# HGRN and retention on one Trainium2 core: k scaled on GpSimd, level 32 copied by ScalarE, the retention gate on GpSimd, head outputs transposed later

## The chip, the core and the metric

The kernel runs on one core of a Trainium2 chip. The core has TensorE (PE, with its weight loads PEld), VectorE (DVE), ScalarE (ACT), GpSimd (POOL) and SyncE (SP, which issues most DMAs). Each engine works through its own list of instructions in order and waits on semaphores for the others. The metric is the device time of one execution in microseconds, the median of several runs.

## What is computed

One layer of a decoder trunk over 1024 positions of width 1024, all in float32: a token-mixing sub-layer (an HGRN2 gated linear recurrence with 8 heads and a retention branch with 4 heads, merged by gates) and a squared-ReLU MLP, each with a residual and a layer norm. The change touches the two recurrent branches:

```python
def _hgrn2(q, zf, v, g, lb):
    q = jax.nn.silu(q)
    log_f = jnp.logaddexp(jnp.log(lb), jnp.log1p(-lb) + jax.nn.log_sigmoid(zf))
    k = (1.0 - lb) * jax.nn.sigmoid(-zf)
    ...
        b = jnp.cumsum(lfc, axis=2)
        rel = jnp.where(causal, b[:, :, :, None, :] - b[:, :, None, :, :], -jnp.inf)
        scores = jnp.einsum('bhid,bhijd,bhjd->bhij', qc, jnp.exp(rel), kc)
        o = scores @ v + (qc * jnp.exp(b)) @ state
        state = exp(b_last) * state + (kc * jnp.exp(b_last - b))^T @ vc
    o = _head_norm(o, centered=False)
    return o * jax.nn.silu(g)

def _retention(q, k, v, g, positions):
    ...
    o = _head_norm(o, centered=True)
    return o * jax.nn.silu(g)

def _head_norm(o, centered):
    if centered:
        o = o - jnp.mean(o, axis=-1, keepdims=True)
    return o * lax.rsqrt(jnp.mean(jnp.square(o), axis=-1, keepdims=True) + HEAD_NORM_EPS)
```

## The kernel before

**Order of the work.** The kernel is one Python trace over tiles. Projections (`dense_T`, helpers `split` and `mm3` at L181 to L188) split each float32 operand into a high and a low part (ACT makes the high, DVE the low part) and multiply three times on PE. The order in which each engine executes its list is settled at compile time by a planner that starts an instruction when, by its own prices for operations, the inputs are ready; it can therefore put a few projection products between two steps of a recurrence. On the chip each list is then in order. In the program's text, generators give the coarse order: `weave` and `mix` alternate the steps of the recurrence (`h_rec`, one `yield` a step) with steps of projections (`h_fill`, later `r_first`). `later(n, fn)` puts a piece of work off by n steps, and `tick`, once a step, runs what is due.

**HGRN.** There are four pairs of heads (p = 0 to 3). For each head `h_rec` keeps k, transposed, as a tile of 128 channels x 1024 positions (named `fk`), q in three versions (`hq`), and builds the 128 x 128 score blocks of eight chunks in S without a cumulative sum: first the pairs of neighbours (L815 to L819), then three levels of sizes 2, 8 and 32 (`H_SIZES`), each of which scores the quarters of a block of 4 x size against each other. One level is:

- L840 and L841 make the moving operand X (tile `U`) from the query product of the level before; L843 and L844 make the products of the decays (tiles `D`);
- four banks of matmuls (L851, two chunks each; the weights are k, the moving operand is X) into PSUM tiles `psa`, of which there are two;
- for each bank three masked copies from PSUM into S (L858, `copy_predicated`, on DVE);
- L861 and L862 scale parts of k by decays for the next level, L863 and L864 do so for X.

Before the levels L824 makes X's query part and L827 scales the even positions of k. After the last level the head goes through its two halves of four chunks: k is transposed (L874) and copied by ACT (L876), the outputs are formed from S and the state (L885, L886), copied by ACT (L887) and squared (L888), and the state is updated (L891, DVE at L896). At the end of a half POOL raises the mean square to the power -1/2 (L901, with `rs` as output), ACT scales the four output blocks (L903), and `h_out` is put off by `H_DEFER[p // 3]` steps: it transposes the half (L911, bank `psb`), multiplies by the gate on DVE (L913) and stores it by a DMA that POOL issues (L914, `oh_d`). `h_merge` reads `oh_d` after the last pair.

**Retention.** `r_head` runs over eight blocks of 128 positions for each of four heads: the state's matmuls (L1105), its high and low parts (ACT and DVE, tiles `fk`), the output's matmuls (L1119), a copy with a scale (L1121), and `r_norm`: statistics on DVE (L1142 to L1144), the power on POOL (L1145), (output - mean) x gate in one DVE instruction (L1146), the scale by the power on ACT (L1147). Three steps later `r_out` transposes the block (L1154), copies it (L1156) and POOL issues its store (L1157). Head 0 runs beside the gate projections, head 1 starts during the last HGRN pair, heads 1 to 3 run beside the merge of the HGRN output (`r_fill`).

Two rows of other places are used for prices: L1221, a product of two SBUF tiles on POOL in the last merge, and L1302, a 128x1 operation on DVE in the norm of the output projection, behind a power on POOL at L1240.

Of the kernel before, what the change touches and what calls it, by code (L numbers as in the profile page):

```python
# [14 lines left out]
AF = mybir.ActivationFunctionType  # L15
ALU = mybir.AluOpType
# [3 lines left out]
P = 128  # L20
# [35 lines left out]

ADA_ORDER = [(s, g) for s in (S_GATE2, S_GATE1, S_SCALE2, S_SHIFT2) for g in range(4)]

H_DEFER = (3, 8)


def constants():
# [70 lines left out]
class Trunk:  # L133
# [666 lines left out]
    def h_rec(self, p, hd):  # L800
        nc = self.nc
        h = 2 * p + hd
        s = self.hst[p][hd]
        q, f, k, v = s["q"], s["f"], s["k"], s["v"]
        S = [self.hS[(2 * h + hf) % len(self.hS)] for hf in (0, 1)]
        V = nc.vector
        fv = f.rearrange("p (b two) -> p two b", two=2)
        V.tensor_tensor(q[:, 2], q[:, 1], fv[:, 1], op=ALU.mult)
        yield

        for bk in range(4):
            pa = self.ps("a", (P, 384)).rearrange("p (c w b) -> p c w b", c=2, w=3)
            for c in (0, 1):
                n = 2 * bk + c
                nc.tensor.matmul(pa[:, c], k[:, n * P:(n + 1) * P], q[:, :, n * 64:(n + 1) * 64], start=True, stop=True)  # L815
            Sv = S[bk // 2][:, bk % 2 * 2:bk % 2 * 2 + 2, :].rearrange("p c (b two) -> p c two b", two=2)
            mk = self.mask8[:, :P].rearrange("p (b two) -> p two b", two=2).unsqueeze(1).to_broadcast([P, 2, 2, 64])
            V.copy_predicated(Sv, mk, pa[:, :, 0:2])
            V.copy_predicated(Sv[:, :, 1], self.mask8[:, P:P + 64].unsqueeze(1).to_broadcast([P, 2, 64]), pa[:, :, 2])  # L819
            if bk == 1:  # L820
                yield
        X = self.hX
        qp = X[:, 0]
        V.tensor_tensor(qp.rearrange("p (b two) -> p two b", two=2), q[:, 0::2],  # L824
                        fv[:, 0].unsqueeze(1).to_broadcast([P, 2, T // 2]), op=ALU.mult)
        ke = k.rearrange("p (b two) -> p two b", two=2)[:, 0]
        V.tensor_tensor(ke, ke, fv[:, 1], op=ALU.mult)  # L827
        Dt = self.hD[hd]
        V.tensor_tensor(Dt, fv[:, 0], fv[:, 1], op=ALU.mult)


        for ln, sz in enumerate(H_SIZES):
            B = T // (4 * sz)
            Xv = X.rearrange("p w (b f s) -> p w f b s", f=4, s=sz)
            kv = k.rearrange("p (b f s) -> p f b s", f=4, s=sz)
            Dv = Dt.rearrange("p (b f) -> p f b", f=4)
            D2 = self.xp.tile([P, 2 * B], F32, tag=f"D{2 * ln + 1}", bufs=1, name=self.uid("D"))
            D4 = self.xp.tile([P, B], F32, tag=f"D{2 * ln + 2}", bufs=1, name=self.uid("D"))
            by = lambda d, *sh: (d if len(sh) == 2 else d.unsqueeze(1).to_broadcast([P, 2, B])).unsqueeze(len(sh)).to_broadcast([P, *sh])
            V.tensor_tensor(Xv[:, 1, 2], Xv[:, 0, 3], by(Dv[:, 2], B, sz), op=ALU.mult)  # L840
            V.tensor_tensor(Xv[:, 1, 1::2], Xv[:, :, 2], by(Dv[:, 1], 2, B, sz), op=ALU.mult)  # L841
            D2v = D2.rearrange("p (b two) -> p two b", two=2)
            V.tensor_tensor(D2v, Dv[:, 0::2], Dv[:, 1::2], op=ALU.mult)  # L843
            V.tensor_tensor(D4, D2v[:, 0], D2v[:, 1], op=ALU.mult)  # L844
            yield
            for bk in range(4):
                pa = self.ps("a", (P, 384))
                for c in (0, 1):
                    n = 2 * bk + c
                    mv = X[:, :, n * P:(n + 1) * P].rearrange("p w (b r) -> p b w r", r=4 * sz)[:, :, :, sz:]  # L850
                    nc.tensor.matmul(pa[:, c * 192:(c + 1) * 192].rearrange("p (b w r) -> p b w r", w=2, r=3 * sz),  # L851
                                     k[:, n * P:(n + 1) * P], mv, start=True, stop=True)
                pv = pa.rearrange("p (b w r s) -> p b w r s", w=2, r=3, s=sz)
                Sv = S[bk // 2][:, bk % 2 * 2:bk % 2 * 2 + 2, :].rearrange("p c (b f s) -> p (c b) f s", f=4, s=sz)
                for j, (dst, src) in enumerate(((Sv[:, :, 1::2], pv[:, :, 0, 0::2]), (Sv[:, :, 2:4], pv[:, :, :, 1]),
                                                (Sv[:, :, 2:4], pv[:, :, 1, 0::2]))):
                    o = P + 64 + 384 * ln + 128 * j
                    V.copy_predicated(dst, self.mask8[:, o:o + 128].rearrange("p (b two s) -> p b two s", two=2, s=sz), src)  # L858
                if bk == 1:
                    yield  # L860
            V.tensor_tensor(kv[:, 0::2], kv[:, 0::2], Dv[:, 1::2].unsqueeze(3).to_broadcast([P, 2, B, sz]), op=ALU.mult)  # L861
            V.tensor_tensor(kv[:, 0:2], kv[:, 0:2], by(D2v[:, 1], 2, B, sz), op=ALU.mult)  # L862
            V.tensor_tensor(Xv[:, 0, 1], Xv[:, 0, 1], by(Dv[:, 0], B, sz), op=ALU.mult)  # L863
            V.tensor_tensor(Xv[:, 0, 2:4], Xv[:, :, 2], by(D2v[:, 0], 2, B, sz), op=ALU.mult)  # L864
            Dt = D4
        yield
        state = None
        for hf in (0, 1):
            g = self.e2()
            nc.sync.dma_start(g, self.hg_d[h][:, hf * 512:hf * 512 + 512])  # L870
            pb = self.ps("b")
            for c in range(4):
                cs = slice(hf * 512 + c * P, hf * 512 + c * P + P)
                nc.tensor.transpose(pb[:, c * P:(c + 1) * P], k[:, cs], self.ident)  # L874
            kt = self.e2()
            nc.scalar.activation(kt, pb, AF.Copy)  # L876
            ob, sq = (self.e2().rearrange("p (c e) -> p c e", c=4) for _ in (0, 1))
            ms = self.xp.tile([P, 4], F32, tag="ms", bufs=2, name=self.uid("ms"))
            for c in range(4):
                n = 4 * hf + c  # L880
                cs = slice(n * P, n * P + P)
                vn = v[:, n, hd * P:(hd + 1) * P]
                po = self.ps("c", (P, P))
                if n > 0:
                    nc.tensor.matmul(po, qp[:, cs], state, start=True, stop=False)  # L885
                nc.tensor.matmul(po, S[hf][:, c, :], vn, start=n == 0, stop=True)  # L886
                nc.scalar.activation(ob[:, c, :], po, AF.Copy)  # L887
                nc.scalar.activation(sq[:, c, :], ob[:, c, :], AF.Square, accum_out=ms[:, c:c + 1])  # L888
                if n < 7:
                    pu = self.ps("c", (P, P))  # L890
                    nc.tensor.matmul(pu, kt[:, c * P:(c + 1) * P], vn, start=True, stop=True)  # L891
                    ns = self.xp.tile([P, P], F32, tag="st", bufs=2, name=self.uid("st"))
                    if n == 0:
                        nc.vector.tensor_copy(ns, pu)
                    else:
                        nc.vector.scalar_tensor_tensor(ns, state, Dt[:, n:n + 1], pu, op0=ALU.mult, op1=ALU.add)  # L896
                    state = ns
                yield
            nc.vector.tensor_scalar(ms, ms, 1.0 / P, HEAD_EPS, op0=ALU.mult, op1=ALU.add)
            rs = self.xp.tile([P, 4], F32, tag="rs", bufs=2, name=self.uid("rs"))  # L900
            nc.gpsimd.tensor_tensor(rs, ms, self.mhalf[:, :4], op=ALU.pow)  # L901
            for c in range(4):
                nc.scalar.activation(ob[:, c, :], ob[:, c, :], AF.Copy, scale=rs[:, c:c + 1])  # L903
            self.later(H_DEFER[p // 3], lambda ob=ob, hf=hf, g=g: self.h_out(h, hf, ob, g))
            yield
# [232 lines left out]
    def r_norm(self, h, n, of, g):  # L1138
        nc, V = self.nc, self.nc.vector
        stat = self.xp.tile([P, 16], F32, tag="stat", bufs=2, name=self.uid("stat"))  # L1140
        b6, mv, rs = stat[:, 0:6], stat[:, 8:10], stat[:, 12:13]
        V.bn_stats(b6, of)  # L1142
        V.bn_aggr(mv, b6)
        V.tensor_scalar(rs, mv[:, 1:2], HEAD_EPS, None, op0=ALU.add)  # L1144
        nc.gpsimd.tensor_tensor(rs, rs, self.mhalf[:, :1], op=ALU.pow)  # L1145
        V.scalar_tensor_tensor(of, of, mv[:, 0:1], g, op0=ALU.subtract, op1=ALU.mult)  # L1146
        nc.scalar.activation(of, of, AF.Copy, scale=rs)  # L1147
        self.later(3, lambda: self.r_out(h, n, of))

    def r_out(self, h, n, of):  # L1150
# [574 lines left out]
```

## Time and profile before

| what | us |
|---|---|
| time, median of 3 runs | 2324.97 |
| lowest and highest | 2318.06, 2326.09 |
| the profiled execution | 2319.84 |
| its span, first to last instruction | 2318.1 |

| engine | busy in the span | share |
|---|---|---|
| PE matmul | 2250.6 | 97% |
| PE weight loads | 1851.3 | 80% |
| DVE | 1652.0 | 71% |
| ACT | 1008.7 | 44% |
| POOL | 294.6 | 13% |

The profile is of one execution. A row of a group of instructions names the line of the kernel, the engine, the operation, the output and input tiles, the shape and the count; behind the bar stand the busy time, the mean length of one in ns, and how long the engine stood idle just before them, with what ended that. A row of a timeline has the start, the length, the engine and line, and in brackets the idle time before it. Matmuls overlap in the pipeline, so the lengths of single ones add up to more than the time that they take, and a busy PE isn't PE at its peak. The HGRN recurrence occupies about 884 to 1240 us of the span, retention heads 1 to 3 about 1240 to 1460 us.

### The profile page before, as it was taken

The page shows a single profiled execution, that of the slowest core. Times are in us where ns is not written, and L with a number is a line of the kernel's source. Part 1 is how long each engine was busy: PE and PEld are TensorE (multiplying, and loading weights), DVE is VectorE, ACT ScalarE, POOL GpSimd, SP SyncE. Part 2 cuts the span into 40 slices and gives each one's busy share as a digit, 9 for nine tenths or more (in the row PEclk, how much of TensorE's full clock was granted, in tenths as well). Part 3 has the DMA queues.
Part 4 walks back from the last instruction along what each step waited for, and adds up shares of the span by engine and source line. Part 5 has one row for each costly group of instructions (what it writes and reads, how often), then busy time and mean ns, then how long its engine had stood idle before and what let it go on. Part 6 is the DMA issues. An engine that isn't in the chain of part 4 may idle for free.

```text
span 2318.1 us, 29884 instructions
## 1 busy us (share of the span) xinstructions
PE 2250.6 (97%) x10366; PEld 1851.3 (80%) x10366; DVE 1652.0 (71%) x3078; ACT 1008.7 (44%) x1829; POOL 294.6 (13%) x460
## 2 busy tenths in 40 slices
PE   6999999999999999999989999999989999999997
PEld 5888888888888788778877788888878888788886
DVE  7866768676777556778876667667886666668669
ACT  4433435443333352432435556222465555643441
POOL 0111010111111120010011222013012111100001
PEclk9999999999999999999999999999999999999999
DMA  9676655433333441122234666864244444777653
GB/s 287 220 229 219 224 195 200 159 129 108 116 109 112 164 150 60 42 91 63 75 104 156 236 193 211 297 212 154 95 145 164 154 152 152 283 254 241 211 168 127
DMA packets 227415, 385.86 MB, mean 166 GB/s; under 512 B 17480, under 2 KB 122688, under 8 KB 226496
## 3 DMA queue, kind: packets, MB, share of 16 engines
q1 hardware_dynamic: 197232, 285.95, 38.7%
q0 software_dynamic: 29712, 97.55, 11.3%
q8 instruction: 82, 1.34, 0.2%
q14 instruction: 69, 0.57, 0.1%
q10 hardware_dynamic: 320, 0.45, 0.1%
HBM read 282.17 MB, written 101.72 MB: 166 GB/s over the span
## 4 chain that ended last, share of the span: by engine, by line
PE 62%; issue 23%; DVE 6%; DMA 3%; POOL 3%; ACT 2%; SPq 0%; ACTq 0%; POOLq 0%; DVEq 0%
PE psd L187 11%; PE psd L186 11%; PE psd L188 11%; PE psa L188 3%; PE psa L187 3%; PE psa L186 3%; PE psc L187 3%; PE psc L186 3%; PE psc L188 3%; PE psb L1119 2%; PE psc L1105 1%; PE psb L186 1%; PE psb L187 1%; PE psb L188 1%; DVE U L182 1%
## 5 line engine op out<-in xcount | busy, mean ns | idle before, releaser
L186 PE MATMUL psd<-U,wh 128*128 128x512 f32 x760 | 305.1, 403 | 2.1 <-ACT wh L181 1.5
L187 PE MATMUL psd<-U,wh 128*128 128x512 f32 x760 | 303.8, 400 | 1.4 <-DVE U L182 1.4
L188 PE MATMUL psd<-U,wl 128*128 128x512 f32 x760 | 303.4, 399 | 0.0
L181 ACT ACTIVATE bh<-s 128x512 fp32r<-128x512 f32 x204 | 128.3, 633 | 248.3 <-PE psd L187 61.1
L186 PE MATMUL psd<-U,bh 128*128 128x512 f32 x496 | 193.8, 391 | 2.1 <-DVE e L449 2.1
L188 PE MATMUL psd<-U,bl 128*128 128x512 f32 x496 | 193.7, 390 | 0.0
L187 PE MATMUL psd<-U,bh 128*128 128x512 f32 x496 | 193.5, 390 | 0.0
L182 DVE TENSOR_TENSOR bl<-raw,bh 128x512 fp32r<-128x512 f32 x153 | 104.6, 689 | 121.4 <-ACT bh L181 121.2
L181 ACT ACTIVATE bh<-raw 128x512 fp32r<-128x512 f32 x153 | 96.9, 636 | 216.3 <-PE psd L187 88.8
L182 DVE TENSOR_TENSOR bl<-s,bh 128x512 fp32r<-128x512 f32 x204 | 139.4, 687 | 69.1 <-ACT bh L181 69.1
L186 PEld LDWEIGHTS psd<-U,wh 128*128 128x128 f32 x760 | 143.1, 189 | 31.0 <-ACT U L181 1.9
L187 PEld LDWEIGHTS psd<-U,wh 128*128 128x128 f32 x760 | 143.8, 189 | 28.6 <-DVE U L182 2.8
L188 PEld LDWEIGHTS psd<-U,wl 128*128 128x128 f32 x760 | 144.0, 189 | 27.6 <-DVE wl L182 0.4
L181 ACT ACTIVATE wh<-raw 128x512 fp32r<-128x512 f32 (+1 forms) x87 | 61.7, 730 | 200.5 <-PE psd L187 174.0
L181 ACT ACTIVATE U<-hr 128x512 fp32r<-128x512 f32 x112 | 70.6, 630 | 157.2 <-issue 69.3
L186 PEld LDWEIGHTS psd<-U,bh 128*128 128x128 f32 x496 | 93.6, 189 | 22.2 <-DVE e L449 2.8
L188 PEld LDWEIGHTS psd<-U,bl 128*128 128x128 f32 x496 | 93.4, 188 | 19.6
L187 PEld LDWEIGHTS psd<-U,bh 128*128 128x128 f32 x496 | 93.5, 189 | 19.4
L182 DVE TENSOR_TENSOR U<-hr,U 128x512 fp32r<-128x512 f32 x112 | 76.8, 686 | 44.4 <-ACT U L181 44.0
L186 PE MATMUL psa<-U,bh 128*128 128x512 f32 x248 | 97.7, 394 | 4.6 <-ACT bh L181 4.3
L188 PE MATMUL psa<-U,bl 128*128 128x512 f32 x248 | 97.5, 393 | 1.0 <-DVE bl L182 1.0
L187 PE MATMUL psa<-U,bh 128*128 128x512 f32 x248 | 97.4, 393 | 0.0
(404 smaller groups left out, 5578.1 us busy)
## 6 DMA issues: line engine op xcount, KB each, us to landing
raw<-in_w_in SPq DMA_DIRECT2D x146, 512.0 KB
raw<-in_w_down SPq DMA_DIRECT2D x48, 512.0 KB
raw<-in_w_ada SPq DMA_DIRECT2D x32, 512.0 KB
raw<-in_w_up SPq DMA_DIRECT2D x32, 512.0 KB
raw<-in_w_pb SPq DMA_DIRECT2D x20, 512.0 KB
adw<-in_w_ada SPq DMA_DIRECT2D x16, 512.0 KB
v_d<-e POOLq DMA_DIRECT2D x32, 256.0 KB, 4.4
rg_d<-e POOLq DMA_DIRECT2D x32, 256.0 KB, 2.6
```

Source lines behind the costliest of these rows:

```text
L181: self.nc.scalar.activation(hi, src, AF.Copy)
L182: self.nc.vector.tensor_tensor(lo, src, hi.bitcast(F32), op=ALU.subtract)
L186: r = mm(out, wh, uh, start=start, stop=False, skip_group_check=more)
L187: mm(out, wh, ul, start=False, stop=False, skip_group_check=more)
L188: return r, mm(out, wl, uh, start=False, stop=stop, skip_group_check=more)
L1105: mm(G[e], l[:, n % 2, es], r, start=n == 0 and i == 0, stop=i == 2, skip_group_check=n > 0)
L1119: mm(po, l, r, start=i == 0, stop=i == len(pairs) - 1)
```

## The change

Four edits:

1. `H_DEFER` goes from (3, 8) to (6, 8): the outputs of pairs 0 to 2 are transposed six steps after their half instead of three.
2. The scalings of k, before the levels (L827) and in each level (L861, L862), are issued on GpSimd instead of VectorE.
3. In the level of 32 the three masked copies of a bank on VectorE become four plain copies on ScalarE, each of 32 partitions: at that size the masks are whole blocks of 32 partitions.
4. In `r_norm` the one product with mean and gate on VectorE becomes a 128x1 product on VectorE (-mean x rs), an ACT instruction with scale and bias in place of the one with a scale, and a product with the gate on GpSimd.

```diff
-H_DEFER = (3, 8)
+H_DEFER = (6, 8)
@@ h_rec
         ke = k.rearrange("p (b two) -> p two b", two=2)[:, 0]
-        V.tensor_tensor(ke, ke, fv[:, 1], op=ALU.mult)
+        nc.gpsimd.tensor_tensor(ke, ke, fv[:, 1], op=ALU.mult)
@@ h_rec, behind the matmuls of a bank
+                if sz == 32:
+                    sv, qv = Sv, pv.rearrange("p b w r s -> p b (w r) s")
+                    for r0, dst, src in ((0, slice(1, 2), slice(0, 1)), (64, slice(3, 4), slice(2, 3)), (32, slice(2, 4), slice(1, 5, 3)),
+                                         (0, slice(2, 4), slice(3, 6, 2))):
+                        nc.scalar.activation(sv[r0:r0 + 32, :, dst], qv[r0:r0 + 32, :, src], AF.Copy)
+                    if bk == 1:
+                        yield
+                    continue
@@ h_rec, at the end of a level
-            V.tensor_tensor(kv[:, 0::2], kv[:, 0::2], Dv[:, 1::2].unsqueeze(3).to_broadcast([P, 2, B, sz]), op=ALU.mult)
-            V.tensor_tensor(kv[:, 0:2], kv[:, 0:2], by(D2v[:, 1], 2, B, sz), op=ALU.mult)
+            G = nc.gpsimd
+            G.tensor_tensor(kv[:, 0::2], kv[:, 0::2], Dv[:, 1::2].unsqueeze(3).to_broadcast([P, 2, B, sz]), op=ALU.mult)
+            G.tensor_tensor(kv[:, 0:2], kv[:, 0:2], by(D2v[:, 1], 2, B, sz), op=ALU.mult)
@@ r_norm
-        V.scalar_tensor_tensor(of, of, mv[:, 0:1], g, op0=ALU.subtract, op1=ALU.mult)
-        nc.scalar.activation(of, of, AF.Copy, scale=rs)
+        nm = stat[:, 14:15]
+        V.scalar_tensor_tensor(nm, mv[:, 0:1], -1.0, rs, op0=ALU.mult, op1=ALU.mult)
+        nc.scalar.activation(of, of, AF.Identity, scale=rs, bias=nm)
+        nc.gpsimd.tensor_tensor(of, of, g, op=ALU.mult)
```

## The prediction

> **What bounds the kernel now.** I read the page first, for the busy shares.
>
> ```profile
> span 2318.1 us, 29884 instructions
> PE 2250.6 (97%) x10366; PEld 1851.3 (80%) x10366; DVE 1652.0 (71%) x3078; ACT 1008.7 (44%) x1829; POOL 294.6 (13%) x460
> ```
>
> TensorE (PE) is busy for 97% of the span. Every part of the change moves work among the other three engines, so only what makes PE wait counts. The second view is the busy time in stretches: the HGRN recurrence (884 to 1240 us) and the retention heads 1 to 3 (1240 to 1460).
>
> ```profile
> 884.00:1240.00 356.00, 339.36 (x1778) 282.66 (x1777) 274.79 (x707) 122.70 (x355) 30.57 (x39) 0.99 0.21 69
> 1240.00:1460.00 220.00, 213.96 (x1054) 173.99 (x1053) 146.07 (x257) 128.17 (x221) 51.70 (x73) 1.00 0.66 222
> ```
>
> The columns are length, PE, PE weight loads, DVE, ACT, POOL (GpSimd), granted clock. PE is idle 356.00 - 339.36 = 16.6 us in the first and 6.0 us in the second: what the change can win from waits lies near 20 us. DVE has 81 us free in the recurrence; it is no bound by sum. The third view is PE's waits, first of the recurrence, then (last two rows) of the retention stretch.
>
> ```profile
> PE psb L911 <- ACT e L903: 7.1, 9, 1.7
> PE psa L851 <- DVE U L841: 4.5, 1, 4.5
> PE psb L874 <- DVE fk L862: 1.4, 2, 0.8
> PE psc L1105 <- ACT e L1075: 4.3, 3, 2.6
> PE psa L1154 <- ACT U L1147: 0.2, 1, 0.2
> ```
>
> The largest is L911, the transposes of a finished head half. The timeline shows two of them:
>
> ```profile
> 934.68 1.03 POOL L901 TENSOR_TENSOR rs<-ms,small 128x4 f32<-128x4 f32 x1 [67.24 <-DVE ms L899]
> 936.20 0.33 PE L911 MATMUL psb<-cst,e 128*128 128x128 f32 x1 [0.90 <-ACT e L903]
> 988.11 1.81 POOL L901 TENSOR_TENSOR rs<-ms,small 128x4 f32<-128x4 f32 x1 [3.06 <-DVE ms L899]
> 990.41 0.62 PE L911 MATMUL psb<-cst,e 128*128 128x128 f32 x2 [1.75 <-ACT e L903]
> 992.02 2.77 PE L851 MATMUL psa<-U,fk 128*128 128x192 f32 x8
> ```
>
> PE's order is fixed at compile time, with L911 where its input should be ready; the power on POOL takes 1.03 us and PE stands 0.90; where it takes 1.81, PE stands 1.75. So the planner prices this POOL operation at almost nothing. That will matter again.
>
> **The change, part by part.** Durations from the groups of lines (whole span for L1221 and the retention, the recurrence for the others):
>
> ```profile
> L858 DVE COPY_PREDICATED U<-mask,psa 128x128 f32<-128x128 uint8 x288 | 77.9, 314 | 26.6 <-PE psa L851 23.9
> L827 DVE TENSOR_TENSOR fk<-fk,fk 128x512 f32<-128x512 f32 x8 | 5.8, 725 | 0.0
> L861 DVE TENSOR_TENSOR fk<-fk,D 128x512 f32<-128x512 f32 x16 | 10.9, 684 | 0.0
> L861 DVE TENSOR_TENSOR fk<-fk,hq 128x512 f32<-128x512 f32 x8 | 5.6, 701 | 0.0
> L862 DVE TENSOR_TENSOR fk<-fk,D 128x512 f32<-128x512 f32 x24 | 16.6, 692 | 0.0
> L887 ACT ACTIVATE e<-psc 128x128 f32<-128x128 f32 x60 | 16.3, 272 | 16.7 <-PE psc L886 16.0
> L911 PEld LDWEIGHTS psb<-cst,e 128*128 128x128 f32 x56 | 7.7, 139 | 13.9 <-ACT e L903 13.2
> L1145 POOL TENSOR_TENSOR stat<-stat,small 128x1 f32<-128x1 f32 x32 | 24.3, 760 | 25.1 <-DVE stat L1144 24.8
> L1146 DVE SCALAR_TENSOR_TENSOR U<-U,stat,e 128x512 f32<-128x512 f32 x32 | 23.8, 744 | 0.4 <-DMA e<-rg_d 0.4
> L1147 ACT ACTIVATE U<-U,stat 128x512 f32<-128x512 f32 x32 | 23.2, 724 | 27.7 <-POOL stat L1145 23.3 <-DVE U L1146 4.3
> ```
>
> *Head outputs six steps later (pairs 0 to 2).* L911, DVE's L913 and POOL's issue of the store L914 move together. By then the power and the four ACT scalings have long ended, so the wait goes. The price lies between PE's own idle time, 7.1 us plus the slow L851 group behind the longest wait (2.77 against 1.54 us for the same eight instructions at 1047.32 below), 8.3 together, and the 13.2 us that the weight loads of L911 stood, 14.4 with that group. I take 13, near the upper end, because the four transposes also arrive at ACT's pace, which PE's idle time doesn't count. Nothing is pushed later that matters: the store is read by the merge after the last pair, whose own deferral of 8 stays. What comes next on PE is a projection product or a level's matmul.
>
> *k on POOL.* Off DVE: 8 + 24 + 24 operations, 5.8 + 10.9 + 5.6 + 16.6 = 38.9 us. Onto POOL: 56 of them. Their nearest row is the only large POOL product, L1221, same shape:
>
> ```profile
> 1548.45 1.22 DVE L182 TENSOR_TENSOR wl<-raw,wh 128x1024 fp32r<-128x1024 f32 x1
> 1548.61 2.20 POOL L1221 TENSOR_TENSOR U<-U,e 128x512 f32<-128x512 f32 x1 [1.38 <-DVE U L1220]
> 1553.14 0.68 DVE L1218 TENSOR_TENSOR U<-U,psd 128x512 f32<-128x512 f32 x1
> 1553.30 1.29 POOL L1221 TENSOR_TENSOR U<-U,e 128x512 f32<-128x512 f32 x1 [2.49 <-DVE U L1220]
> 1553.85 1.28 DVE L1220 TENSOR_TENSOR U<-U,e 128x512 f32<-128x512 f32 x1
> ```
>
> It takes 1.29 us beside a DVE operation that reads PSUM, and 2.20 when DVE is in a product of two SBUF operands: 1548.45 + 1.22 = 1549.67, and 1.14 after that is its end, so it had waited. The reverse shows too: L1220, of the shape of L862 (0.69 us), takes 1.28 and ends 0.54 after the POOL operation does. So the two exclude each other; 56 operations cost 72 us (at 1.29) to 123 (at 2.20) of POOL, which has 325 free there. The price lies in the chain from one level to the next:
>
> ```profile
> 1047.32 1.54 PE L851 MATMUL psa<-U,fk 128*128 128x192 f32 x8
> 1049.49 0.68 DVE L861 TENSOR_TENSOR fk<-fk,D 128x512 f32<-128x512 f32 x1
> 1050.10 0.29 DVE L858 COPY_PREDICATED U<-mask,psa 128x128 f32<-128x128 uint8 x1
> 1050.29 0.68 DVE L862 TENSOR_TENSOR fk<-fk,D 128x512 f32<-128x512 f32 x1
> 1050.89 0.42 DVE L863 TENSOR_TENSOR U<-U,D 128x256 f32<-128x256 f32 x1
> 1052.55 0.69 DVE L841 TENSOR_TENSOR U<-U,D 128x512 f32<-128x512 f32 x1
> 1053.47 0.81 PE L851 MATMUL psa<-U,fk 128*128 128x192 f32 x4
> ```
>
> From the end of the level's matmuls (1048.86) to X ready (1053.24) it is 4.4 us; PE starts the next level 0.23 later and spends the time between on projection products, not idle. After the change POOL's two products can start at once, beside the masked copies (which read PSUM). But L863 to L841 (1050.89 to 1053.24, 2.35 us) are products from SBUF and exclude them: 0.1 + 2 x 1.29 + 2.35 = 5.0 us, to 1053.9, some 0.65 later than now. Where projection products fill PE this is hidden: cost 0 if the order allows for it. Where there are none (the one wait of 4.5 us above) it is +0.6. The waits on L862 (1.4) stay about as they are. DVE, 39 us lighter, may win the same back elsewhere. I take 0, with ends of -3 and, if the order doesn't allow for it, +35 (below). The first product, L827, has no such chain behind it: L824 and L829 to L841 run on DVE meanwhile.
>
> *Level 32 on ACT.* Off DVE: a third of L858, 26 us. Onto ACT: 8 heads x 4 banks x 4 copies = 128, each smaller than L887's 0.272: at most 35 us, and ACT has 233 free. A bank is released after 4 x 0.27 = 1.1 us instead of 3 x 0.31 = 0.94; over 32 banks that is 0 to 5 us, hidden by the products between the two bank pairs: 0.
>
> *Retention's gate on POOL.* L1146 (0.74) leaves DVE, a 128x1 operation comes. The kernel has the same one in its output norm:
>
> ```profile
> L1302 DVE SCALAR_TENSOR_TENSOR stat<-stat x8: 159/160/163, 1605.6 to 1682.3; 128x1 f32<-128x1 f32 x8
> DVE stat L1302 <- POOL stat L1240: 6.0, 8, 0.8
> ```
>
> It takes 0.16 us, but DVE stands 0.75 before it for POOL's power, and what is queued behind it on DVE waits (the low parts of the state, which PE needs). So DVE gains nothing: 0.74 against 0.91. The chain to L1154 was power (0.76; L1146 beside it) and L1147 (0.72); it becomes power, 0.16, 0.72, and a POOL product of 1.29: 1.45 us longer. Three steps of deferral cover it except where they are just enough, as at 1266:
>
> ```profile
> 1265.86 0.72 ACT L1147 ACTIVATE U<-U,stat 128x512 f32<-128x512 f32 x1 [0.43 <-DVE U L1146]
> 1266.64 0.66 PE L1154 MATMUL psa<-cst,U 128*128 128x128 f32 x4 [0.20 <-ACT U L1147]
> ```
>
> I allow for up to five such places of 1.45 us, 0 to 7, and take 0, as PE's total wait there is 0.2 us today.
>
> **Sum.** -13 + 0 + 0 + 0 = -13 us. The profiled execution took 2319.84 us around its span of 2318.1; that lies 5 below the median of the runs shown, 2324.97. I forecast from the median: **2312 us**, with 2302 to 2322 for this case (deferral -8 to -14, DVE's -3, retention's +5, and some 5 us between runs).
>
> **Rivals.**
>
> *1. The exclusion isn't in the plan: slower.* PE's order is made from planned durations, and the rows of L901 show POOL underpriced. A planner that knows no exclusion has the copies end 0.61 earlier (no L861 among them, 1049.78) and X ready 2.35 later, at 1052.13. The chip needs until 1053.9. PE would stand 1.7 us at each of 16 turns (two per head): 27 us. At the eight turns to the key transposes (L874), the two POOL products and L863 with L864 (1.0) exclude each other: about 1 us each, 8. 35 - 13 + 2 or 3 for the retention = +25: **2350 us**. For it: the two POOL rows of L901, and that DVE's and PE's times meet to 0.2 us today, so there is no reserve. Against it: a planner that prices POOL's large product at 2 us or more would leave the room unknowingly. It decides from 13 / 24 = 0.55 us a turn upwards. The Trainium skill, "SBUF — State Buffer", section "Who interferes with whom", states it as a rule: a VectorE instruction with two SBUF inputs and a GpSimd instruction that reads SBUF take turns on an exclusive lock, for the whole instruction. The rows of 1548 and 1553 agree.
>
> *2. The wait moves.* Without L911's wait PE reaches the next input sooner, and stands there: L851 has 0.2 us of reserve. Then nothing is won: **2325 us**. Against it: DVE's chain starts with PE's own matmuls, so it moves along with them.
>
> *3. A lighter DVE shortens the stretch with few products (after 1160) as well:* 4.5 + 1.4 us of waits and the slow clock behind them: another -12: **2300 us**. The exclusion speaks against it.
>
> **How the numbers follow.** Forecast 0.48, rival 1 0.30, rival 2 0.12, rival 3 0.10. About 0.5% (11.6 us) is what a measurement of this kernel can tell from no change, and the forecast lies just beyond it: of its 0.48, 0.30 counts as faster and 0.18 as same. Rival 1 gives 0.28 slower, 0.02 same; rival 2 0.10 same, 0.02 slower; rival 3 is faster. Together: faster 0.40, same 0.30, slower 0.30. The range reaches from rival 3 to rival 1: 2298 to 2350; it leaves out the upper part of rival 1 (0.10) and a little below.
>
> **What would show it.** PE's waits no longer list L911 on ACT. L861 and L862 appear on POOL: near 1.3 us each if they rarely meet DVE, towards 2.2 if they do. If L851 or L874 wait for POOL or for L841 in two dozen places, rival 1 holds. ACT's busy time in the recurrence grows by about 30 us, DVE's falls by about 60. In the retention DVE waits for L1145 32 times, some 0.75 us each. If DVE's waits reach PE through the state's low parts, I am wrong there.

## The result and the profile after

The changed kernel took 2361.36 us (2357.79 to 2362.44, four runs) against 2322.26 us (2318.06 to 2326.09, four runs) of the kernel before, taken side by side. The medians lie 39 us apart; the ratio is 1.0175 with a 95% interval of [1.016, 1.0189]. The forecast of 2312 us and its range, which ended at 2350, were both missed, on the side of the first rival. The kernel before is put at about 2320 us below: its median in each series of experiments lay between 2318.9 and 2320. Behind a ratio, the us are that ratio on 2320 us; where the two medians alone give another figure, it is named.

The page after, its span and its busy times:

```profile
span 2360.3 us, 30007 instructions
PE 2256.9 (96%) x10366; PEld 1849.8 (78%) x10366; DVE 1626.3 (69%) x2926; ACT 1039.9 (44%) x1957; POOL 406.2 (17%) x548
```

PE has the same 10366 instructions. DVE lost only 25.7 us of busy time, although 38.9 us of k, 26 us of masked copies and 23.8 us of L1146 have left it and only 32 products of 128x1 came: something on DVE became slower. The lines of the kernel have moved: L858 is L866 after the change, the new copies of level 32 are L859, L861 to L864 are L870 to L873, L874 is L883, L887 is L896, L891 is L900, L901, L903 and L911 are L910, L912 and L920; in the retention L1105 is L1114, L1145 and L1147 are L1154 and L1157, the new product with the gate is L1158, and L1154 is L1165. L815 to L851 keep their numbers.

Where the time went is seen from two groups of matmuls that frame the stretches: L815 starts each of the eight heads, L1105 (L1114) is the retention state's product. The rows give count, shortest, median and longest in ns, then the start of the first and of the last in us; first the two rows of the kernel before,

```profile
L815 PE MATMUL psa<-hq,fk x128: 323/326/401, 898.2 to 1205.3; 128*128 128x192 f32 x128
L1105 PE MATMUL psc<-e,U x168: 387/393/502, 799.5 to 1435.3; 128*128 128x512 f32 x168
```

then the same two of the changed kernel.

```profile
L815 PE MATMUL psa<-hq,fk x128: 323/326/402, 903.7 to 1242.1; 128*128 128x192 f32 x128
L1114 PE MATMUL psc<-e,U x168: 387/389/628, 804.0 to 1478.0; 128*128 128x512 f32 x168
```

The retention frame grew from 635.8 to 674.0 us, by 38.2 of the 42.2 us that the span is longer. Inside it the heads' frame, seven head periods, grew from 307.1 to 338.4 us: 31.3, or 4.5 us a head. The 4.5 us ahead of the first L1114 lie before any edited instruction has run, since `r_norm` and the heads come behind it, and are left out of the account.

PE's waits after the change (total in us, times, longest):

```profile
PE psa L851 <- DVE U L841: 19.1, 16, 1.6
PE psb L883 <- POOL fk L871: 12.3, 8, 1.5
...
PE psa L851 <- POOL fk L827: 5.9, 8, 1.0
PE psc L900 <- ACT e L896: 5.2, 7, 0.8
...
PE psa L1165 <- POOL U L1158: 2.6, 5, 0.8
...
PE psc L1114 <- ACT e L1084: 2.1, 3, 1.0
...
PE psc L1114 <- DVE e L1085: 1.7, 3, 0.8
...
PE psa L851 <- ACT U L859: 1.6, 8, 0.2
```

A row of the kernel before that the prediction doesn't show:

```profile
PE psc L891 <- ACT e L887: 0.8, 1, 0.8
```

The counts after are those of a loop: 16 turns between levels, 8 turns from the last level to the key transposes, 8 first matmuls of the levels. Against the rows of before, L841's wait grew by 14.6, that of the key transposes (L874 there) by 10.9, and L827, L859 and L1158 are new. The wait of L911 for L903 (7.1) is no longer listed; L900's wait for ACT has come in its place.

One turn between two levels, in the timeline after:

```profile
1055.82 1.54 PE L851 MATMUL psa<-U,fk 128*128 128x192 f32 x8
...
1057.52 1.54 POOL L870 TENSOR_TENSOR fk<-fk,hq 128x512 f32<-128x512 f32 x1 [3.55 <-PE psa L851]
1058.11 1.26 DVE L872 TENSOR_TENSOR U<-U,hq 128x256 f32<-128x256 f32 x1
...
1059.14 1.34 POOL L871 TENSOR_TENSOR fk<-fk,D 128x512 f32<-128x512 f32 x1
...
1059.47 1.56 DVE L873 TENSOR_TENSOR U<-U,D 128x512 f32<-128x512 f32 x1
...
1061.52 0.69 DVE L841 TENSOR_TENSOR U<-U,D 128x512 f32<-128x512 f32 x1
...
1062.36 1.54 PE L851 MATMUL psa<-U,fk 128*128 128x192 f32 x8 [1.32 <-DVE U L841]
```

Read the ends: POOL's L870 ends at 1059.06, and DVE's L872, which began 0.95 us earlier, ends 0.31 later. L871 ends at 1060.48, L873 0.55 after that. The two engines take turns, and the DVE products L872 and L873 take 2.82 us together. Before the change L863 took 0.42 in the turn shown there, and L864 0.69 in the mean:

```profile
L864 DVE TENSOR_TENSOR U<-U,D 128x512 f32<-128x512 f32 x24 | 16.5, 689 | 0.0
```

L841, with no POOL work beside it, has its old length of 0.69. PE reaches the next level 1.32 us too early: its list has fewer projection products at this place than the chip's time would take.

How many fewer can be counted in the traces. Over the 16 turns between two levels, PE's list has 21.3 other matmuls in the mean before the change, nearly all of projections, and 17.4 after it, while the time from the end of a level's matmuls to the end of L841 (X ready) went only from 4.8 to 5.0 us. So the chain hardly became longer, although two products had left DVE; what shrank is the room that the plan gave it.

### The profile page after: what moved, and what is told of

The parts are those of the page before. It is cut to its first block, busy times and chain, and to the rows that moved or that the text cites. A ratio compares the mean times of both kernels' runs of the same rounds, so it can differ in the third digit from the quotient of the medians.

```text
span 2360.3 us, 30007 instructions
## 1 busy us (share of the span) xinstructions
PE 2256.9 (96%) x10366; PEld 1849.8 (78%) x10366; DVE 1626.3 (69%) x2926; ACT 1039.9 (44%) x1957; POOL 406.2 (17%) x548
## 3 DMA queue, kind: packets, MB, share of 16 engines
q8 instruction: 82, 1.34, 0.2%
## 4 chain that ended last, share of the span: by engine, by line
PE 42%; DVE 8%; issue 6%; POOL 3%; DMA 2%; ACT 2%; SPq 0%; DVEq 0%; POOLq 0%; ACTq 0%
PE psd L187 8%; PE psd L186 8%; PE psd L188 8%; PE psa L851 2%; PE psa L188 2%; PE psa L186 2%; PE psa L187 2%; PE psc L188 1%; PE psc L187 1%; PE psc L186 1%; DVE U L182 1%; PE psb L1128 1%; DVE U L873 1%; DVE U L866 1%; PE psc L1114 1%
## 5 line engine op out<-in xcount | busy, mean ns | idle before, releaser
L851 PE MATMUL psa<-U,fk 128*128 128x192 f32 x384 | 76.2, 337 | 26.7 <-DVE U L841 19.1
L186 PE MATMUL psa<-U,bh 128*128 128x512 f32 x248 | 97.7, 394 | 4.1 <-ACT bh L181 3.8
```

Of the source, the lines that this page charges most:

```text
L186: r = mm(out, wh, uh, start=start, stop=False, skip_group_check=more)
```

## The experiments

Each is the kernel before with the edit named, unless it says otherwise; each ratio is to runs of the kernel before on the same chip. The theory after the result: **POOL's reads and DVE's two-operand products exclude each other, the plan of PE's order knows neither this nor POOL's real durations, so X and k come late at every turn.** Rivals: the other edits lose the time; or any long POOL step in the chain does it, without the exclusion.

### One edit at a time

**Head outputs later** (`H_DEFER` alone):

```diff
-H_DEFER = (3, 8)
+H_DEFER = (6, 8)
```

> The kernel before with the one edit H_DEFER (6, 8). If the deferral wins what the prediction gave it (13 us), the time falls to 0.9944 of before, PE's wait of L911 on ACT (7.1 us in 9 waits) goes and nothing comes in its place. If the wait only moves (the power on POOL still stands in ACT's list, and the output copy L887 of the next chunk behind it), PE waits some 5 us at L891 on L887 instead and the time falls by 3 to 7 us, 0.997 to 0.9985.

2319.1 us, 0.9994 [0.9985, 1.0004]: no change, which neither of the two expectations had. PE's wait list of this kernel still has

```profile
PE psb L911 <- ACT e L903: 6.9, 9, 1.0
```

and its timeline shows the transposes at the same distance from the power as before (936.20 there, 0.49 after the power's end at 935.71):

```profile
940.01 1.04 POOL L901 TENSOR_TENSOR rs<-ms,small 128x4 f32<-128x4 f32 x1 [67.20 <-DVE ms L899]
...
941.53 0.33 PE L911 MATMUL psb<-cst,e 128*128 128x128 f32 x1 [0.90 <-ACT e L903]
```

0.48 us after the power's end, with the same 0.90 us of standing. Of the 12 halves whose step was changed, 10 have their first transpose behind as many matmuls of the recurrence as before. Six program steps or three make next to no difference here to where this work stands in PE's list, which fits a planner that starts an instruction when, by its prices, the input is ready.

**All of k on GpSimd** (L827, L861 and L862 with `nc.gpsimd` in place of `V`):

> The kernel before with k scaled on GpSimd alone (the product before the levels and both in each level). Theory 1 (the scaling of k on GpSimd is the loss, by its products and VectorE's excluding each other and by PE's order not allowing for it): 35 to 50 us slower, 1.015 to 1.021, with PE waiting at L851 for L841 16 times and at L874 for L862 eight times. Theory 2 (the loss comes from the copies on ScalarE or from the retention gate): within 10 us of before.

2350.61 us, 1.0135 [1.012, 1.0149]: 31 us, a little under the 35 to 50 expected and most of the loss. PE's waits:

```profile
PE psa L851 <- DVE U L841: 20.4, 16, 1.9
PE psb L874 <- POOL fk L862: 8.8, 8, 1.4
...
PE psa L851 <- POOL fk L827: 6.9, 7, 1.2
```

These are the three rows of the changed kernel, with nearly the same counts. Their 36 us, less the 5.9 of the first two before, are 30. Against that, the wait of L911 for L903 falls from 7.1 to 3.6 us in this kernel, without any deferral; the profiled execution, the shortest of its four, is 26 us over the profiled one of before.

**Level 32 copied by ScalarE** (the block `if sz == 32` alone):

> The kernel before with the level of 32 copied by ScalarE alone. Theory 1: within 5 us of before, PE waiting for the copies some 0.2 us a head (1.6 us in all). Theory 2: 15 us slower or more.

2321.83 us, 1.0009 [0.9999, 1.0018]: 0 to 4 us.

**The retention's gate on GpSimd** (the four lines of `r_norm` alone):

> The kernel before with the retention gate on GpSimd alone. Theory 1: 0 to 7 us slower (PE's five waits at the block transposes, 2.6 us in the profile after). Theory 2: 15 us slower or more.

2324.49 us, 1.0026 [1.0014, 1.0038]: 3 to 9 us (4.6 by the medians). The profile shows little of it. The frame of the state's matmuls is 635.9 us (801.4 to 1437.3) against 635.8, and the transposes (L1156 here) wait for the product:

```profile
PE psa L1156 <- POOL U L1149: 1.9, 3, 0.8
```

The profiled execution was the shortest of its six (2321.96), so it can miss a part of what the others show; where the 6 us lie stays open.

### Exclusion, or only a long step

**Idle POOL work that reads SBUF.** k stays on DVE. POOL multiplies two 128x128 parts of v into a scratch tile six times a level, at about the moment at which the products of k would run; ACT touches the scratch tile first, so that POOL starts behind the last bank. Nothing reads the result.

```diff
+            scr = self.xp.tile([P, P], F32, tag="scr", bufs=1, name=self.uid("scr"))
+            nc.scalar.activation(scr[:, :1], pa[:, :1], AF.Copy)
+            for _ in range(6):
+                nc.gpsimd.tensor_tensor(scr, v[:, 0, :P], v[:, 1, :P], op=ALU.mult)
```

> The kernel before, k on VectorE, with idle work on GpSimd: after each level ScalarE copies one column of the last bank into a scratch tile, and six products of 128x128 from SBUF write that tile; nothing reads it. Exclusion theory (a GpSimd product from SBUF and a VectorE product of two SBUF inputs shut each other out): VectorE's L861 to L864 and L841 get longer than their 0.69 us, PE waits at L851 for L841 at most of the 16 turns, 15 to 35 us slower. Price theory (PE waits only because k itself comes late from an engine that the planner underprices): VectorE's products stay at 0.69 us and the time within 4 us of before.

2333.99 us, 1.0065 [1.0048, 1.0082]: 15 us. DVE's product and PE's wait in the recurrence (L868 is the L864 of the kernel before):

```profile
L868 DVE TENSOR_TENSOR U<-U,D 128x512 f32<-128x512 f32 x24 | 21.0, 873 | 0.0
```

```profile
PE psa L851 <- DVE U L841: 15.9, 14, 5.6
```

**The same with writes only:** twelve memsets of the scratch tile in place of the six products.

> The same idle work, but twelve fills of the scratch tile in place of the six products: GpSimd is as busy and reads nothing. Exclusion theory: VectorE's products stay at 0.69 us, the time within 4 us of before, unlike the kernel with products. If any work on GpSimd beside VectorE costs (or the column copied by ScalarE does), it is as slow as that one.

2318.39 us, 0.9998 [0.9988, 1.0008]. POOL's memsets and DVE's product:

```profile
L864 POOL MEMSET scr<- 128x128 f32 x288 | 59.0, 205 | 183.7 <-ACT scr L862 168.7
...
L868 DVE TENSOR_TENSOR U<-U,D 128x512 f32<-128x512 f32 x24 | 16.5, 688 | 0.0
```

POOL work that no instruction waits for costs 15 us (11 to 19) when it reads SBUF and nothing when it only writes. Where it reads, DVE's products are longer (0.87 for 0.69 us) and PE's wait for L841 is 11.4 us more than before; ACT's copy of one column is in both kernels. Each level has some 2.5 us of writes (59.0 / 24); a later control writes for longer. On this the Trainium skill, "SBUF — State Buffer", section "Who interferes with whom", states that a VectorE instruction with two SBUF inputs contends with a GpSimd instruction that reads SBUF, and not with one that only writes it. The two runs agree.

**The levels' k alone on POOL** (L861 and L862; L827 stays on DVE):

> Only the two products of k in each level on GpSimd; the first scaling of k stays on VectorE. If the parts add up, the loss is that of all k products less that of the first scaling: 31 - 5 = 26 us, ratio 1.011, with waits of L851 for DVE L841 near 20 us in 16 places and of L874 for POOL near 9 us in 8. If the first scaling is what starts the chain late, the loss falls to under 15 us.

2342.5 us, 1.0103 [1.0088, 1.0118]: 24 us. PE's waits:

```profile
PE psa L851 <- DVE U L841: 22.1, 16, 1.6
PE psb L874 <- POOL fk L862: 8.6, 8, 1.1
```

**The same places in k written by memsets.** This is the control for "any long POOL step". The kernel leaves out the scaling of k in the levels, so it takes the same two products off DVE as the kernel of the levels' k alone, and POOL writes where it would have multiplied.

```diff
-            V.tensor_tensor(kv[:, 0::2], kv[:, 0::2], Dv[:, 1::2].unsqueeze(3).to_broadcast([P, 2, B, sz]), op=ALU.mult)
-            V.tensor_tensor(kv[:, 0:2], kv[:, 0:2], by(D2v[:, 1], 2, B, sz), op=ALU.mult)
+            for kw in (kv[:, 0::2], kv[:, 0::2], kv[:, 0:2], kv[:, 0:2], kv[:, 0:2]):
+                nc.gpsimd.memset(kw, 0.5)
```

> Leaves out the scaling of k in the levels: GpSimd instead writes constants over the same parts of k, in five memsets a level, which read nothing. GpSimd is then as much in the chain of k as with the products, and DVE is as much lighter. If turn-taking of the two engines makes the loss, DVE's L863 keeps its 0.69 us, the waits of L851 for L841 go (under 3 us in all) and the time is within 0.5% of before, or up to 10 us below it since DVE has two products fewer in each chain. If a long GpSimd step in k's chain is enough, L851 and L874 wait for GpSimd's memsets and the loss stays above 15 us.

2321.32 us, 1.0008 [0.9998, 1.0017]: 0 to 4 us. One turn in the timeline:

```profile
1041.15 3.32 POOL L862 MEMSET fk<- 128x512 f32 x5 [5.69 <-PE psa L851]
1041.83 0.44 DVE L863 TENSOR_TENSOR U<-U,hq 128x256 f32<-128x256 f32 x1
...
1042.37 0.72 DVE L864 TENSOR_TENSOR U<-U,D 128x512 f32<-128x512 f32 x1
...
1043.58 0.69 DVE L841 TENSOR_TENSOR U<-U,D 128x512 f32<-128x512 f32 x1
```

POOL writes the next level's k for 3.32 us, longer than the two products of the changed kernel take (2.96 from 1057.52 to 1060.48), and DVE's products beside it keep their lengths. PE's waits:

```profile
PE psa L851 <- DVE U L841: 1.5, 1, 1.5
...
PE psb L874 <- POOL fk L862: 0.7, 1, 0.7
```

So a long POOL step in k's chain doesn't by itself cost the 24 us. One thing differs besides the reads, how the planner prices a memset. The room that the plan left can be counted: between two levels PE's list has 17.1 other matmuls in the mean here and 16.3 with the levels' k on POOL, nearly the same. X is ready 3.6 us behind a level's matmuls here and 4.9 there. X is made by DVE's products alone, so it is their time on the chip that differs, not the plan's room.

**The first scaling of k alone** (L827 on POOL):

> The kernel before with only the product before the levels (L827) on GpSimd, the scaling in the levels back on VectorE. Price theory for this one product: it takes 1.5 us where PE's order has room for some 0.6, so PE waits 0.9 us at the first L851 of each head: 6 to 8 us slower, 1.0025 to 1.0035. The prediction had 0 for it.

2325.18 us, 1.0022 [1.0012, 1.0031]: 5 us, a little under the 6 to 8 expected.

```profile
PE psa L851 <- POOL fk L827: 5.9, 7, 1.3
```

Here no exclusion is needed: beside L827 DVE is mostly in masked copies from PSUM. In the changed kernel L827 takes 1.51 us where DVE took 0.73, and PE's first matmul of the levels stands 0.7 us right behind it:

```profile
1051.90 1.51 POOL L827 TENSOR_TENSOR fk<-fk,fk 128x512 f32<-128x512 f32 x1 [5.30 <-PE psa L815]
...
1053.46 1.57 PE L851 MATMUL psa<-U,fk 128*128 128x192 f32 x8 [0.72 <-POOL fk L827]
```

### The edits without k, in pairs

**All but k** (deferral, level 32 and the gate):

> The whole change except k, which stays on VectorE. If the parts add up: -1 + 2 + 6 = +7 us, ratio 1.003 (1.000 to 1.005). If the four edits together make a loss that no single one has, it lies above 1.006.

2331.06 us, 1.0051 [1.0035, 1.0067]: 12 us, more than the 7 of the single runs and under the 1.006 of the other expectation. Two pairs followed.

**Deferral with level 32:**

> Deferral and level 32 on ScalarE together, the rest as before. The three edits without k lost 12 us together and 7 us as a sum of single runs. If deferral and level 32 lose more together than alone (the later program step changes the order once the level's copies no longer hold DVE), ratio 1.003 or more, with over 9 us of waits of the head outputs' transposes. If they only add up: 0.9994 + 0.0009, that is 1.000, up to 1.002.

2323.18 us, 1.0019 [1.0011, 1.0028]: just inside what adding up allowed, though the waits below are over the 9 us of the other expectation.

**Level 32 with the gate:**

> Level 32 on ScalarE and the retention gate on GpSimd, without the deferral. If the loss without k comes from these two meeting (both lengthen what ScalarE does in the stretch where retention head 1 runs beside the last HGRN pair), ratio 1.004 or more. If they only add up: 1.0009 x 1.0026 = 1.0035 by the medians, or 1.000 if the gate's share was one between runs, as its profile says, where the first to the last of the state's matmuls took 635.9 us against 635.8 before.

2326.73 us, 1.0029 [1.0018, 1.004]: no more than the two edits add up to.

The wait of the head outputs' transposes (L919 in these kernels) tells the two pairs apart: first with the deferral, then without it.

```profile
PE psb L919 <- ACT e L911: 10.3, 12, 1.2
```

```profile
PE psb L919 <- ACT e L911: 7.0, 8, 1.3
```

With level 32 on ACT the later step does change the list, and for the worse: 12 waits instead of 8, 3.3 us more. The kernel of all but k has the first row too. This may be a part of the extra 5 us; the times alone don't tell it from adding up, since 5 us is about as much as the intervals together, and the rest stays open.

### What would have removed the wait

**Transposes held behind the head's matmuls.** `H_DEFER` as changed, and an order without a semaphore on PE: for pairs 0 to 2 the first transpose of a half comes behind the last recurrence matmul (L851 or L891) that the program had issued by then. (`behind` is the kernel's own helper for such an order.)

```diff
+            m = nc.tensor.transpose(pb[:, c * P:(c + 1) * P], ob[:, c, :], self.ident)
+            if c == 0 and h < 6:
+                self.behind(m, self.h_last)
```

> The kernel before with H_DEFER (6, 8) and, for pairs 0 to 2, an order on PE's own list: a half's transposes L911 come behind the last level or state matmul issued when they are due. If the deferral alone did nothing because PE's list is made by readiness and puts L911 0.5 us behind the power whatever the step, this takes the wait away: L911 starts 3 us or more behind the power, and the time falls by 7 to 14 us, 0.994 to 0.997. If the wait moves to the next reader of ScalarE (L891 on L887), it falls by 3 us or less.

2315.5 us, 0.9975 [0.9965, 0.9984]: 5.8 us below before (3.7 by the medians), between the two expectations, and the one kernel here that is clearly faster than the one before. L911 no longer waits (7.1 us before). Some 3 us come back as PE's wait for a copy on ACT:

```profile
PE psc L891 <- ACT e L887: 3.8, 6, 0.8
```

It was 0.8 in the kernel before. The timeline of this kernel shows why:

```profile
940.06 1.28 ACT L903 ACTIVATE e<-e,rs 128x128 f32<-128x128 f32 x4 [1.35 <-POOL rs L901]
...
941.55 0.49 PE L891 MATMUL psc<-U,e 128*128 128x128 f32 x2 [0.78 <-ACT e L887]
...
943.34 0.60 PE L911 MATMUL psb<-cst,e 128*128 128x128 f32 x4
```

ACT's list is in order too. Its four scalings (L903) stand 1.35 us for POOL's power, and the copies L887 of the next half are queued behind them; PE needs those.

## Why the prediction was wrong

**What bounds the kernel** held: only what makes PE wait counts. Moving 26 us of copies from DVE to ACT cost 2 us, and the loss of the whole change is PE's waits. Those listed with the result, with the rows of before taken off, come to 14.6 (L841) + 10.9 (L883) + 5.9 (L827) + 4.4 (L900) - 7.1 (L911) + 2.4 (L1165) + 1.6 (L859) - 2.2 + 1.7 (L1114) = 32.2 of the 38.2 us. Two rows not listed there bring it to 35.0: L815 for L819 (0.8 before, 2.5 after) and the load in front of L1048 (3.5 and 4.6).

**k on POOL: "I take 0" failed, and with it the choice between forecast and rival 1.** The prediction had both ends of the price, 0 and +35, and took the one on the condition that "the order allows for it", while its own row, PE standing 1.75 us behind a power of 1.81, said that POOL's prices weren't to be relied on. The measured cost is 31 us, with k alone. The rival's terms, against the changed kernel:

- 16 turns between levels at 1.7 us, 27: came in 16 places, 1.2 us each, 19.1. The plan saw X ready too early; that is shown by the counts of matmuls in PE's list and by the memset control.
- 8 turns to the key transposes, about 1 us each, 8: came as 12.3, and as 8.8 with k alone.
- L827, which "has no such chain behind it": **wrong**. The argument looked at DVE's chain alone. L827 writes k, which is the weight of the very next L851, and POOL takes twice as long as DVE did. 5.9 us, shown by the run with L827 alone.

The duration was bounded well: 1.21 to 1.30 us for most of these POOL products, against 1.29 and 2.20 predicted. What wasn't bounded was DVE's side. The groups of the changed kernel in the recurrence:

```profile
L873 DVE TENSOR_TENSOR U<-U,D 128x512 f32<-128x512 f32 x24 | 37.0, 1543 | 0.0
...
L871 POOL TENSOR_TENSOR fk<-fk,D 128x512 f32<-128x512 f32 x24 | 31.2, 1299 | 1.9
```

L873 (L864 there) took 0.69 before, and DVE's busy time fell by 25.7 us in the whole span, where the prediction looked for about 60 in the recurrence alone. The reckoning of 5.0 us from the end of a level's matmuls to X ready was good, since 1057.36 to 1062.21 in the turn shown is 4.85 and the mean of the 16 turns is 5.0: the mistake was not the length of the chain but whether PE's list knew it.

**Deferral: -13 failed.** "L911, DVE's L913 and POOL's issue of the store L914 move together" supposed that a program step moves work in PE's list. The run with the deferral alone gives 0 with the wait of 6.9 us still there. In the changed kernel the wait did go, but k on POOL alone had already halved it, so this isn't the deferral's doing alone. There L900 stands behind the same power by way of ACT, 5.2 us, the same sequence as in the timeline of the held transposes (at 942.65 the scalings L912 start, 1.35 us late for the power, and at 944.14 L900, 0.77 late for the copy behind them). That is rival 2's "the wait moves", by a path (ACT's list) that the prediction didn't name. The size was wrong too. Of the two prices, 8.3 us from PE's own idle time and 14.4 from the standing of its weight loads, the forecast leaned to the second; with the order forced, 5.8 us are won, less than either.

**Level 32: 0 with an end of +5** held: +2 alone, which is not clear of nothing. Its wait is L851 for L859, 1.6 us in eight places of 0.2.

**Retention: 0 with an end of +7** came near its end, +6 alone by the ratio (+4.6 by the medians). The "five such places" came as five waits of L1165, but they are 2.6 us and not 7, and the rest isn't found in the trace. DVE's stand for the power, foreseen at 0.75 us 32 times, is there:

```profile
DVE stat L1156 <- POOL stat L1154: 21.9, 25, 1.2
```

The prediction named what would prove it wrong here, that these waits reach PE through the state's low parts: they do, but as 1.7 us only (L1114 for DVE's L1085), while its waits for ACT there fell by 2.2.

**Rival 3, a lighter DVE,** had no chance beside the exclusion. The memset control shows what it would be worth, as DVE does two products fewer there in each turn:

```profile
L815 PE MATMUL psa<-hq,fk x128: 323/326/402, 901.3 to 1195.7; 128*128 128x192 f32 x128
```

The frame of the heads is 12.7 us shorter than before (294.4 for 307.1), close to that rival's figure, but the frame of the retention around it is the same (802.6 to 1438.5, 635.9 for 635.8): what the heads win is given back later. In that control the 12 us are no gain.

So the sum, by the single runs, is -1 + 31 + 2 + 6 = +38, where the change gave +39 by the medians and +41 by its ratio, and in two parts, all but k (+12) and the levels' k and L827 (24 + 5), it is +41. The sign and four fifths of the size come from one term.

## What to carry to other kernels

Before an elementwise product goes to GpSimd, look at what VectorE does at that moment. Where it is in products of two SBUF operands, one engine stands while the other works, and here the chain gained nothing (4.8 us to X ready before, 5.0 after). A GpSimd step that only writes had no such price here, and neither had VectorE's masked copies from PSUM (0.31 us before, 0.32 after). Where a planner settles the order, ask of each edit whether the planner's price for it is the chip's. Here a chain that took as long as before became a wait of PE at each of 16 turns, because the plan counted on a shorter one. A later step in the program need not move anything in such a list. An explicit order on the engine did, and then the next in-order list (here ACT's) has to be looked through for what is queued behind the same wait.

## What the runs showed of the hardware

- The price of a POOL product goes with the patterns of its operands: the same 128x512 multiplication took 1.51 us for L827, which takes every second position, and 1.54 for L870 in the first level, but 1.21 for L870 in the later levels; on DVE these forms were alike (0.725, 0.701 and 0.684 us). Which operand does it isn't shown for L870: in the first level L871 takes runs of two positions of k as well, with another pattern of the decays, and its median there was 1.34, although it began there while DVE's L872 was still running.

```profile
L870 POOL TENSOR_TENSOR fk<-fk,hq 128x512 f32<-128x512 f32 x8 | 12.4, 1545 | 30.0 <-PE psa L851 25.9 <-DVE U L866 4.1
L870 POOL TENSOR_TENSOR fk<-fk,D 128x512 f32<-128x512 f32 x16 | 19.3, 1207 | 101.2 <-PE psa L851 88.2 <-issue 6.7 <-DVE U L866 6.2
```

- The power on POOL became quicker when its neighbour left: 0.760 us in the mean before, with the product L1146 beside it on DVE, and 0.617 after. With the gate's edit alone it took 0.610.

```profile
L1154 POOL TENSOR_TENSOR stat<-stat,small 128x1 f32<-128x1 f32 x32 | 19.8, 617 | 24.0 <-DVE stat L1153 23.7
```

- The engine that comes first goes on, and the other can stand for long. In the run with idle reads, POOL's first product of one level began 0.03 us behind a DVE product. Seven DVE products of two SBUF operands followed each other without a gap until 1053.76, each of 0.41 or 0.68 us, and POOL's product ended 0.32 us after the last of them, 4.31 us after its start; the quickest of these products took 0.45. The row has the six of that level:

```profile
1049.77 7.26 POOL L864 TENSOR_TENSOR scr<-U 128x128 f32<-128x128 f32 x6 [4.55 <-ACT scr L862]
```
